# State products of a bidirectional S5 layer: factors as weights and chunk inputs moving, in place of chunk inputs as weights

## The chip, the cores and the metric

The kernel runs on one core of a Trainium2 chip. The metric is the device time of one execution in microseconds. Three runs of the kernel before took 1600.52, 1600.65 and 1602.56 us (median 1600.65).

## The reference

Two layers of a backbone over 256 latent tokens and 256 context tokens with 1024 channels, all fp32. Layer 0 mixes tokens with a bidirectional diagonal state space (S5), 64 groups of 16 channels with 64 complex states each, and then runs a dense SwiGLU; layer 1 is attention and a top-2-of-8 expert SwiGLU. The change lies in the S5 mixer of layer 0:

```
def _s5_scan(u, a_re, a_im, log_dt, b_re, b_im, s0, reverse):
    lam_re, lam_im, bbar_re, bbar_im = _zoh(a_re, a_im, log_dt, b_re, b_im)
    bu_re = jnp.einsum('bngi,gpi->bngp', u, bbar_re)
    bu_im = jnp.einsum('bngi,gpi->bngp', u, bbar_im)
    ...
    _, _, s_re, s_im = lax.associative_scan(
        _ssm_combine, (a_seq_re, a_seq_im, bu_re, bu_im), reverse=reverse, axis=1)
```

The scan runs over time in both directions (r = 0 forward, r = 1 reverse), context first, then latent tokens. The readout multiplies the states with C, adds a skip term, and a GLU follows.

## The kernel before, in words

Time is cut into 64 chunks of 8 steps. For every chunk and group the kernel computes what the 8 inputs of the chunk add to the state at the end of the chunk (VS), then runs a scan over the 64 chunks on DVE (`scan_range`, L846 to L857), and then computes the outputs from chunk states (`states`, `outer`) and from inputs inside the chunk (`taps`, `windows`, `inner`).

**The inputs.** U (L637 to L642) holds the inputs transposed: 128 partitions (8 steps x 16 channels), 32 slots of 128 columns, 64 columns (chunks) per group.

**The sets.** The 64 groups are worked off in 16 sets of four (`iters`, L570). `z_mul(i)` (L573) forms on DVE three products of lambda powers with B factors, 128 x 512 each (L581). They are the three factors of a complex product with three multiplications; in the sets listed in ZSUM (11 of 16 before) it also adds the first product to the other two (L586). `z_tr(i)` (L589) turns the products with four transposes per factor (L595) and evicts each with ACT into zz (L596): two factors in a ZSUM set, three otherwise. `v_stage(i)` (L652) multiplies: weights are 64 chunk columns of U, and 256 columns of zz move (L662; in a set without sums also the first factor, L661). ACT evicts into vc (L663). `t_stage(i)` (L666) turns vc with four transposes (L674), and ACT evicts the result into VS, the forward half with L677 and the reverse half with two L680.

**What runs beside it.** `w_gen(blk)` (L684) is a generator of 22 DVE pieces, two of 128 x 512 (L687, L689) and twenty of 128 x 1024 (L701 to L709), which form the readout weights W of one half of the groups, in two tensors (wr by L703 and L707, wi by L705 and L709). The list WN says how many pieces are taken in each iteration. FILL lists the eight iterations in which one slice of the modulation matrix is multiplied (`ada_go`: L264 on PE, evicted into R by L270). In the next iteration `ada_done` turns R with four transposes (L284, tile cp), ACT gathers it into part (L285), and after the last of the eight slices DVE reduces part into cols (L290, L292).

**The order.** The loop of L714 issues in iteration i: z_mul(i) and z_tr(i) for i from 2 to 15, ada_done, v_stage(i - 1), t_stage(i - 2), WN[i] pieces of W, ada_go. After it `pin` (L93) fixes the order of the instructions on DVE, ACT and PE as they were issued. Sets 0 and 1 are multiplied and turned before the loop. zq and zz have two buffers each, PSUM eight tiles of 128 x 512.

**Behind the loop.** The pools z (zq, zz, vc) and f are closed, and W1, the readout weights of the second half, is opened at the other end of the same memory. POOL loads dm (L744) into the place of pool f, DVE multiplies it (L746) and runs w_gen(1), and then `scan_range` starts (L888): per chunk L852, L855 and L857, each on the result of the one before. Taps on PE (L779, L784) run beside that.

Of the kernel before, what the change touches and what calls it, by code (L numbers as in the profile page):

```python
# [10 lines left out]
F32 = mybir.dt.float32  # L11
# [3 lines left out]
AF = mybir.ActivationFunctionType  # L15
# [30 lines left out]
WOP = ((13, 13, 17, 17, 18, 19, 20, 20, 21, 21, 22, 22, 24, 24, 24, 24), (29, 29, 30, 30, 31, 32, 33, 34, 35, 35, 36, 36))  # L46
FILL = (3, 5, 6, 7, 9, 10, 11, 13)
LATE = 8
ZSUM = (4, 5, 6, 8, 9, 10, 11, 12, 13, 14, 15)
WN = (0, 6, 1, 2, 1, 1, 2, 2, 2, 2, 1, 4, 2, 1)  # L50


def host_consts():
# [26 lines left out]
def backbone_kernel(ctx: ExitStack, tc: tile.TileContext, x, c, cx, c_ctx, ada_w, ada_b, norm_mix_g, norm_ffn_g,  # L80
# [4 lines left out]
    V, S, T, GP, SY = nc.vector, nc.scalar, nc.tensor, nc.gpsimd, nc.sync  # L85
# [42 lines left out]
    def popen(name, bufs, side):  # L128
        cm = tc.tile_pool(name=name, bufs=bufs, side=side, reuse_waits="tile")
        opened.append(cm)  # L130
        return cm.__enter__(), cm
# [11 lines left out]
    def ps(name="ps"):  # L143
        return ps_pool.tile([128, 512], F32, tag="ps", name=name)
# [45 lines left out]
    z, z_cm = popen("z", 2, "left")  # L190
# [24 lines left out]
    ident = kc[:, 0:128]  # L215
# [89 lines left out]
    def ada_go(ld_=None):  # L305

        if ld_ is None:
            ld_, = ada_next(1)
        ada_open.append((ld_, ada_ev(ada_mm(ld_))))

    def ada_done(late=None):
        while ada_open:
            ada_turn(*ada_open.pop(0), late)
# [17 lines left out]
    for r in range(2):  # L331
        src = bn[:, r].rearrange("g r (p i) -> g (r p) i", i=I)
        for q in range(2):
            t = ps()
# [235 lines left out]
    iters = [(blk, gp) for blk in range(2) for gp in range(8)]  # L570
    zst = {}

    def z_mul(i):  # L573

        blk, gp = iters[i]
        g0 = 32 * blk + 4 * gp
        gs = slice(g0, g0 + 4)
        qs_ = []
        for k, (a, b) in enumerate(((PS_, BB[0]), (PZ[1], tb[1]), (PZ[0], tb[0]))):
            q = z.tile([128, 4, 8, I], F32, name=f"zq{k}", tag=f"zq{k}")  # L580
            V.tensor_tensor(q, a.rearrange("p s g -> p g s")[:, gs, :, None].to_broadcast([128, 4, 8, I]),  # L581
                            b[:, gs, None, :].to_broadcast([128, 4, 8, I]), op=OP.mult)
            qs_.append(q)
        if i in ZSUM:
            for k in (1, 2):
                V.tensor_tensor(qs_[k], qs_[k], qs_[0], op=OP.add)  # L586
        zst[i] = qs_

    def z_tr(i):  # L589
        qs_ = zst[i]  # L590
        zz = z.tile([128, 3, 4, 128], F32, name="zz")
        for k in range(1 if i in ZSUM else 0, 3):
            t = ps()
            for g in range(4):
                T.transpose(t[:, 128 * g:128 * g + 128], qs_[k][:, g].rearrange("p s i -> p (s i)"), ident)  # L595
            S.activation(zz[:, k].rearrange("p g q -> p (g q)"), t, AF.Copy)  # L596
        zst[i] = zz
# [6 lines left out]
    t = ps()  # L604
    T.transpose(t[:, :128], pr, ident)
    S.activation(pcol, t[:, :128], AF.Copy)
    t = ps()
# [22 lines left out]
    for r in range(2):  # L630
        for q in range(2):
            t = ps()
# [5 lines left out]
    for q in range(8):  # L638
        t = ps()
# [9 lines left out]
    VS = s_pool.tile([128, 64, 2, G], F32, name="VS", tag="big")  # L649
    w0, w0_cm = popen("w0", 1, "right")  # L650
    W = [[w0.tile([128, 32, 9, I], F32, name=f"W0{r}") for r in range(2)], None]
    def v_stage(i):  # L652
        blk, gp = iters[i]
        zz = zst[i]
        vc = z.tile([128, 2, 2, 128], F32, name="vc")
        t = ps()
        for g in range(4):
            o = t[64 * (g % 2):64 * (g % 2) + 64, 256 * (g // 2):256 * (g // 2) + 256]
            u = U[:, 8 * g + gp, 64 * blk:64 * blk + 64]
            if i not in ZSUM:  # L660
                T.matmul(o, lhsT=u, rhs=zz[:, 0:1, g, :].to_broadcast([128, 2, 128]), start=True, stop=False)  # L661
            T.matmul(o, lhsT=u, rhs=zz[:, 1:3, g, :], start=(i in ZSUM), stop=True)  # L662
        S.activation(vc.rearrange("p g r q -> p (g r q)"), t, AF.Copy)  # L663
        zst[i] = vc

    def t_stage(i):  # L666
        blk, gp = iters[i]
        g0 = 32 * blk + 4 * gp
        vc = zst.pop(i)
        t = ps()  # L670
        for r in range(2):
            for g in range(2):
                o = 256 * r + 128 * g
                T.transpose(t[:, o:o + 128], vc[:, g, r], ident)  # L674
        tv = t.rearrange("p (r g c) -> p r g c", r=2, g=4)
        vs = VS[:, :, :, g0:g0 + 4].rearrange("p c r g -> p r g c")
        S.activation(vs[0:64], tv[0:64], AF.Copy)  # L677
        for h in range(2):
            a = tv[64:128, :, :, 32 * h + 31:32 * h + 32]
            S.activation(vs[64:128, :, :, 32 * h:32 * h + 32],  # L680
                         bass.AP(tensor=a.tensor, offset=a.offset, ap=[a.ap[0], a.ap[1], a.ap[2], [-1, 32]]), AF.Copy)
# [29 lines left out]

    wgen = w_gen(0)
    n = len(iters)
    for i in range(n + 2):  # L714
        if 2 <= i < n:
            z_mul(i)
            z_tr(i)
        ada_done()
        if 0 <= i - 1 < n:
            v_stage(i - 1)  # L720
        if 0 <= i - 2 < n:
            t_stage(i - 2)
        for _ in range(WN[min(i, len(WN) - 1)]):
            next(wgen, None)
        if i in FILL:
            ada_go()
# [12 lines left out]
    for zz in range(2):  # L739
        rs = slice(64 * zz + 32, 64 * zz + 48)  # L740
        for blk in range(2):
            for gh in range(2):
                o = 512 * blk + 256 * gh + 128 * zz
# [512 lines left out]
    for j in range(2):  # L1256
        for lt in range(2):
# [3 lines left out]
            tv = tab[:, j, lt].rearrange("p o (a j d) -> p o j a d", a=2, j=2)  # L1261
# [33 lines left out]
    for kt in range(KT):  # L1295
        if kt == 2:
            later()
        for j, w in enumerate(w0):
            for tt in range(4):
                o = pts[tt][:, 256 * j:256 * j + 256]  # L1300
                T.matmul(o, lhsT=h[0][:, kt, 128 * tt:128 * tt + 128], rhs=w[0][:, kt, :], start=(kt == 0 and j == 0),
                         stop=False)
                T.matmul(o, lhsT=h[0][:, kt, 128 * tt:128 * tt + 128], rhs=w[1][:, kt, :], start=False, stop=False)
                T.matmul(o, lhsT=h[1][:, kt, 128 * tt:128 * tt + 128], rhs=w[0][:, kt, :], start=False,
                         stop=(kt == KT - 1 and j == 1))
# [377 lines left out]
    n = len(items)  # L1683
# [393 lines left out]
    n = len(chunks)  # L2077
# [49 lines left out]
    with tc.If(nmax > 128):  # L2127
        op_, op_cm = popen("op", 1, "right")
        for e_ in range(NE):
# [8 lines left out]
            for q in range(2):  # L2138
                t = ps()
                for j in range(4):  # L2140
                    for lt in range(2):
                        T.matmul(t[:, 128 * j:128 * j + 128],
                                 lhsT=hf[:, lt, 512 * q + 128 * j:512 * q + 128 * j + 128], rhs=se[:, lt, :],
                                 start=(lt == 0), stop=(lt == 1))
                S.activation(xg[:, 4 * q:4 * q + 4, :].rearrange("p a b -> p (a b)"), t, AF.Copy)
            yp = [ps("py") for _ in range(2)]
            for f in range(DFF // 256):
                t = ps()
                for half in range(2):
                    w = load(moe_gu[0, e_].rearrange("(k p) n -> p k n", p=128)[:, :, DFF * half + 256 * f:  # L2150
                                                                                  DFF * half + 256 * f + 256], [KT, 256])
                    for kt in range(KT):
                        T.matmul(t[:, 256 * half:256 * half + 256], lhsT=xg[:, kt, :], rhs=w[:, kt, :],
                                 start=(kt == 0), stop=(kt == KT - 1))
# [3 lines left out]
                t = ps()  # L2158
# [5 lines left out]
                for j in range(2):  # L2164
                    for n in range(2):
                        T.matmul(yp[n], lhsT=aT[:, 128 * j:128 * j + 128], rhs=w[:, j, 512 * n:512 * n + 512],
                                 start=(f == 0 and j == 0), stop=(f == DFF // 256 - 1 and j == 1))
            so = op_.tile([128, 256], F32, name="so")
            t = ps()
# [3 lines left out]
            for n in range(2):  # L2173
                y, u = [op_.tile([128, 512], F32, name=t_) for t_ in ("y", "u")]
                S.activation(y, yp[n], AF.Copy)
                for lt in range(2):
                    t = ps()
# [37 lines left out]
```

## Time and profile before

| what | value |
|---|---|
| median of three runs | 1600.65 us |
| the profiled execution | 1599.54 us, its span 1597.8 us |
| PE busy | 1482.7 us (93%) |
| DVE busy | 894.0 us (56%) |
| ACT busy | 708.4 us (44%) |
| the loop over sets | about 61 to 136 us |
| the scan over chunks | about 159 to 234 us |

The span is the time from the first to the last instruction; the execution's own time is 1.74 us longer. PE's busy time counts matmuls, whose ends are modelled: consecutive matmuls overlap in it, so the cost of one in a stream is read from starts, not from durations. PEld are the weight loads.

### The profile page before, as it was taken

How to read it: one execution, taken by the hardware profiler on the slowest of the kernel's cores; microseconds unless marked ns; L12 is line 12 of the kernel's file. 1: busy time of each engine (PE TensorE's matmuls, PEld its weight loads, DVE VectorE, ACT ScalarE, POOL GpSimd, SP SyncE). 2: the span in 40 equal slices, each digit the busy share in tenths (PEclk: the TensorE clock that was granted, in tenths of full speed). 3: DMA queues.
4: the chain of work that ended last, by engine and by line, in shares of the span. 5: the costliest groups of instructions: out<-in, count | busy, mean ns of one | idle time of the engine just before them, and what ended most of it. 6: DMA issues, size and time to landing. Idle time of an engine off the chain costs nothing.

```text
span 1597.8 us, 24082 instructions
## 1 busy us (share of the span) xinstructions
PE 1482.7 (93%) x9742; PEld 1046.3 (65%) x9742; DVE 894.0 (56%) x1391; ACT 708.4 (44%) x928; POOL 38.6 (2%) x69
## 2 busy tenths in 40 slices
PE   4897859999999999999899899989998999989995
PEld 3454648768888888878767687447843786357641
DVE  6997994354232333246877876337831785168621
ACT  4687674243212222235575665136621573056500
POOL 1001000000000000001001000000000000000020
PEclk9997889999999999999999899999999999999999
DMA  9682567263232321234442779999999999999996
GB/s 263 228 307 88 157 181 237 79 211 109 95 113 79 106 97 61 87 127 151 168 172 99 245 225 378 405 407 408 406 406 404 409 405 393 403 409 404 402 405 246
DMA packets 167192, 398.49 MB, mean 249 GB/s; under 512 B 12108, under 2 KB 66576, under 8 KB 166944
## 3 DMA queue, kind: packets, MB, share of 16 engines
q1 hardware_dynamic: 164688, 391.61, 66.5%
q0 software_dynamic: 1184, 3.18, 0.8%
q10 hardware_dynamic: 1200, 2.07, 0.6%
q8 instruction: 79, 1.29, 0.3%
q14 instruction: 41, 0.34, 0.1%
HBM read 394.78 MB, written 2.05 MB: 248 GB/s over the span
## 4 chain that ended last, share of the span: by engine, by line
PE 77%; DVE 10%; DMA 5%; ACT 4%; issue 1%; SPq 0%; DVEq 0%; ACTq 0%
PE pgu L982 10%; PE pgu L981 10%; PE pgu L983 10%; PE pgu L1932 8%; DMA raw<-in_moe_w_gate_up_dram 3%; PE pd L981 3%; PE pd L983 3%; PE pd L982 3%; PE py L981 3%; PE py L982 3%; PE py L1995 3%; PE py L983 3%; DVE sq L852 2%; DVE VS L857 1%; DVE sq L855 1%
## 5 line engine op out<-in xcount | busy, mean ns | idle before, releaser
L962 DVE TENSOR_TENSOR lo<-raw,hi 128x2048 fp32r<-128x2048 f32 (+1 forms) x184 | 401.0, 2186 | 209.1 <-ACT hi L962 206.9
L962 ACT ACTIVATE hi<-raw 128x2048 fp32r<-128x2048 f32 (+1 forms) x184 | 337.4, 1834 | 314.0 <-PE pd L982 81.1
L1932 PE MATMUL pgu<-raw,xb 128*32 128x512 f32 (+1 forms) x1536 | 157.0, 558 | 2.1 <-DMA raw<-in_moe_w_gate_up_dram 2.1
L981 PE MATMUL pgu<-hi,xa 128*128 128x512 f32 (+1 forms) x384 | 148.2, 386 | 5.3 <-ACT hi L962 5.3
L982 PE MATMUL pgu<-lo,xa 128*128 128x512 f32 (+1 forms) x384 | 147.2, 383 | 5.5 <-DVE lo L962 5.5
L983 PE MATMUL pgu<-hi,xa 128*128 128x512 f32 (+1 forms) x384 | 146.1, 381 | 0.0
L981 PE MATMUL pgu<-hhi,hi 128*128 128x512 f32 x352 | 137.0, 390 | 0.5 <-ACT hhi L1113 0.5
L982 PE MATMUL pgu<-hlo,hi 128*128 128x512 f32 x352 | 137.1, 389 | 0.0
L983 PE MATMUL pgu<-hhi,lo 128*128 128x512 f32 x352 | 137.0, 389 | 0.0
L1932 PEld LDWEIGHTS pgu<-raw,xb 128*32 128x32 f32 x1536 | 48.4, 110 | 98.7 <-issue 86.6
L981 PEld LDWEIGHTS pgu<-hi,xa 128*128 128x128 f32 x384 | 74.6, 194 | 23.7 <-ACT hi L962 6.0
L982 PEld LDWEIGHTS pgu<-lo,xa 128*128 128x128 f32 x384 | 74.5, 194 | 19.2 <-DVE lo L962 6.4
L1995 PE MATMUL py<-raw,aT 128*32 128x512 f32 x704 | 80.1, 594 | 5.6 <-DMA raw<-in_moe_w_down_dram 5.5
L983 PEld LDWEIGHTS pgu<-hi,xa 128*128 128x128 f32 x384 | 74.3, 193 | 13.8
L981 PEld LDWEIGHTS pgu<-hhi,hi 128*128 128x128 f32 x352 | 66.0, 188 | 15.0 <-ACT hhi L1113 1.4
L982 PEld LDWEIGHTS pgu<-hlo,hi 128*128 128x128 f32 x352 | 66.1, 188 | 14.5 <-DVE ncq L1110 0.8
L983 PEld LDWEIGHTS pgu<-hhi,lo 128*128 128x128 f32 x352 | 66.1, 188 | 13.7
L981 PE MATMUL pd<-act,hi 128*128 128x512 f32 x176 | 70.0, 399 | 0.0
L983 PE MATMUL pd<-act,lo 128*128 128x512 f32 x176 | 69.5, 395 | 0.0
L982 PE MATMUL pd<-act,hi 128*128 128x512 f32 x176 | 69.5, 395 | 0.0
L981 PE MATMUL py<-hi,aT 128*128 128x512 f32 x176 | 69.2, 393 | 0.0
L982 PE MATMUL py<-lo,aT 128*128 128x512 f32 x176 | 69.0, 392 | 0.0
(444 smaller groups left out, 2346.6 us busy)
## 6 DMA issues: line engine op xcount, KB each, us to landing
raw<-in_moe_w_gate_up_dram SPq DMA_DIRECT2D x128, 1024.0 KB, 11.4
raw<-in_moe_w_down_dram SPq DMA_DIRECT2D x88, 1024.0 KB, 10.5
raw<-in_ada_w_dram SPq DMA_DIRECT2D x48, 1024.0 KB, 7.5
raw<-in_moe_w_gate_up_dram SPq DMA_DIRECT2D x64, 768.0 KB, 9.4
raw<-in_ffn_w_gate_up_dram SPq DMA_DIRECT2D x22, 1024.0 KB, 5.2
raw<-in_ssm_glu_w_dram SPq DMA_DIRECT2D x8, 1024.0 KB, 8.3
raw<-in_ffn_w_down_dram SPq DMA_DIRECT2D x8, 1024.0 KB, 5.1
raw<-in_attn_w_qkv_dram SPq DMA_DIRECT2D x6, 1024.0 KB, 5.1
```

What stands on the lines that cost most here:

```text
L852: V.tensor_tensor(t, VS[:, k - 1, None, :, g].to_broadcast([128, 2, 2, g.stop - g.start]), T8[:, :, :, g], op=OP.mult)
L855: V.tensor_tensor(t[:, :, 0, :], t[:, :, 0, :], t[:, :, 1, :], op=OP.add)
L857: V.tensor_tensor(VS[:, k, :, g], VS[:, k, :, g], t[:, :, 0, :], op=OP.add)
L962: ins = [S.activation(hi, r, AF.Copy), V.tensor_tensor(lo, r, hi.bitcast(F32), op=OP.subtract)]
L981: T.matmul(o, lhsT=a[0], rhs=b[0], start=start, stop=False)
L982: T.matmul(o, lhsT=a[0], rhs=b[1], start=False, stop=False)
L983: T.matmul(o, lhsT=a[1], rhs=b[0], start=False, stop=stop)
L1932: T.matmul(pt[64 * j_ + 32 * q:64 * j_ + 32 * q + 32, 0:bw], lhsT=XB[:, kt, o + 32 * q:o + 32 * q + 32], rhs=wj_[j_][:, kk, b:b + bw], sta ...
L1995: T.matmul(yps[e_][0][64 * n + 32 * q:64 * n + 32 * q + 32, :], lhsT=aT[1][:, m, 32 * q:32 * q + 32], rhs=wt_[0][:, kk, ns], start=first, ...
```

## The change

The state products are formed with the turned factors zz as weights (128 columns) and the 64 chunk columns of U moving, so that the result already has states on partitions. vc, its eviction and t_stage are gone. ACT's first eviction into VS is written in the order chunk, part, group. ZSUM shrinks to four sets. WN is changed so that the pieces of W are taken over all sets. The loop starts at 1 and ends one iteration earlier.

```
-ZSUM = (4, 5, 6, 8, 9, 10, 11, 12, 13, 14, 15)
-WN = (0, 6, 1, 2, 1, 1, 2, 2, 2, 2, 1, 4, 2, 1)
+ZSUM = (9, 11, 13, 15)
+WN = (0, 4, 1, 1, 2, 1, 2, 1, 2, 1, 2, 1, 2, 1)
...
     def v_stage(i):
+
         blk, gp = iters[i]
-        zz = zst[i]
-        vc = z.tile([128, 2, 2, 128], F32, name="vc")
-        t = ps()
+        g0 = 32 * blk + 4 * gp
+        zz = zst.pop(i)
+        tv = ps().rearrange("p (r g c) -> p r g c", r=2, g=4)
         for g in range(4):
-            o = t[64 * (g % 2):64 * (g % 2) + 64, 256 * (g // 2):256 * (g // 2) + 256]
             u = U[:, 8 * g + gp, 64 * blk:64 * blk + 64]
             if i not in ZSUM:
-                T.matmul(o, lhsT=u, rhs=zz[:, 0:1, g, :].to_broadcast([128, 2, 128]), start=True, stop=False)
-            T.matmul(o, lhsT=u, rhs=zz[:, 1:3, g, :], start=(i in ZSUM), stop=True)
-        S.activation(vc.rearrange("p g r q -> p (g r q)"), t, AF.Copy)
-        zst[i] = vc
-
-    def t_stage(i):
-        blk, gp = iters[i]
-        g0 = 32 * blk + 4 * gp
-        vc = zst.pop(i)
-        t = ps()
-        for r in range(2):
-            for g in range(2):
-                o = 256 * r + 128 * g
-                T.transpose(t[:, o:o + 128], vc[:, g, r], ident)
-        tv = t.rearrange("p (r g c) -> p r g c", r=2, g=4)
+                T.matmul(tv[:, :, g, :], lhsT=zz[:, 0, g, :], rhs=u[:, None, :].to_broadcast([128, 2, 64]), start=True,
+                         stop=False)
+            for r in range(2):
+                T.matmul(tv[:, r, g, :], lhsT=zz[:, 1 + r, g, :], rhs=u, start=(i in ZSUM), stop=(i in ZSUM or r == 1))
         vs = VS[:, :, :, g0:g0 + 4].rearrange("p c r g -> p r g c")
-        S.activation(vs[0:64], tv[0:64], AF.Copy)
+        S.activation(VS[0:64, :, :, g0:g0 + 4], tv[0:64].rearrange("p r g c -> p c r g"), AF.Copy)
...
-    for i in range(n + 2):
+    for i in range(1, n + 1):
...
-        if 0 <= i - 1 < n:
-            v_stage(i - 1)
-        if 0 <= i - 2 < n:
-            t_stage(i - 2)
+        v_stage(i - 1)
```

## Rows read from the trace of the kernel before

**Rows 1.** Windows: span and busy us (instructions) of each engine, granted clock, DMA.

```profile
61.00:119.00 58.00, 52.74 (x419) 30.61 (x419) 57.45 (x79) 47.08 (x85) 0.00 (x0) 1.00 0.68 243
...
142.00:159.00 17.00, 16.80 (x132) 11.42 (x132) 16.94 (x17) 10.95 (x33) 0.45 (x4) 0.52 0.10 15
```

**Rows 2.** Chain of waits in order of time: start us, us, engine, tile, line.

```profile
130.16 1.23 PE ps L595 x8
...
157.62 1.14 DVE W L709
...
232.08 0.24 DVE VS L857 x2
```

**Rows 3.** Timeline of DVE and POOL: start us, us, instruction, [idle before and its releaser].

```profile
91.27 1.28 DVE L586 TENSOR_TENSOR zq<-zq,zq 128x512 f32<-128x512 f32 x2
92.47 1.21 DVE L707 TENSOR_TENSOR W<-W,n 128x1024 f32<-128x1024 f32 x1
...
126.93 0.42 DVE L290 TENSOR_REDUCE cols<-part 128x64 f32<-128x256 f32 x1 [5.42 <-ACT part L285]
...
134.11 1.23 DVE L703 TENSOR_TENSOR W<-PQ,CD 128x1024 f32<-128x1024 f32 x1 [3.49 <-PE ps L662]
136.55 1.23 DVE L705 TENSOR_TENSOR W<-PQ,CD 128x1024 f32<-128x1024 f32 x1 [1.22 <-PE ps L674]
...
130.02 4.23 POOL L744 DMA_DIRECT2D dm<-in_ssm_d_dram  x8 [120.06 <-DVE zq L586]
```

**Rows 4.** Timeline of PE, the first product and two stretches of the loop.

```profile
61.02 0.66 PE L661 MATMUL ps<-zz,U 128*64 128x256 f32 x4
...
69.69 1.47 PE L595 MATMUL ps<-kc,zq 128*128 128x128 f32 x12
71.09 0.66 PE L661 MATMUL ps<-zz,U 128*64 128x256 f32 x4
...
79.88 1.04 PE L595 MATMUL ps<-kc,zq 128*128 128x128 f32 x8
80.84 1.08 PE L662 MATMUL ps<-zz,U 128*64 128x256 f32 x8
81.86 0.66 PE L674 MATMUL ps<-kc,vc 128*128 128x128 f32 x4
82.45 1.92 PE L264 MATMUL ada<-raw,sc 128*32 128x512 f32 x16
84.30 1.09 PE L595 MATMUL ps<-kc,zq 128*128 128x128 f32 x8
```

**Rows 5.** Timeline of PE, the end of the loop.

```profile
125.88 0.66 PE L284 MATMUL cp<-kc,R 128*128 128x128 f32 x4 [1.14 <-ACT R L270]
...
131.32 1.08 PE L662 MATMUL ps<-zz,U 128*64 128x256 f32 x8
```

**Rows 6.** Timeline of PE, small streams behind weight loads of 128 and 64 columns.

```profile
171.18 0.71 PE L779 MATMUL ps<-W,bd 128*64 128x144 f32 x8
171.82 0.29 PE L784 MATMUL ps<-dm,kc 16*64 16x16 f32 x4
...
853.71 1.85 PE L1599 MATMUL plt<-rw,xT 128*128 128x8 f32 x16
855.42 0.47 PE L981 MATMUL pw<-hi,oT 128*128 128x512 f32 x1
```

**Rows 7.** Timeline of PE, two gaps and what ran behind the second.

```profile
28.04 3.73 PE L447 MATMUL ps<-ke,L 64*64 64x64 f32 x40 [3.04 <-ACT FT L474]
...
141.90 0.47 PE L779 MATMUL ps<-W,bd 128*64 128x144 f32 x4 [3.59 <-ACT bd L757]
...
153.98 1.11 PE L284 MATMUL cp<-kc,R 128*128 128x128 f32 x4
```

**Rows 8.** Groups by line, shapes kept apart, ACT: busy us, mean ns.

```profile
L677 ACT ACTIVATE VS<-ps 64x512 f32<-64x512 f32 x16 | 17.4, 1089 | 0.0
...
L635 ACT ACTIVATE CT<-ps 128x512 f32<-128x512 f32 x4 | 2.1, 603 | 1.0 <-PE ps L634 1.0
```

## The prediction, blind

> **What bounds the kernel now.** I read the windows first, then the chain of waits, then the timelines of DVE and PE in the stretch that the diff touches. From 61 to 119 us DVE is busy for 57.45 of 58.00 us, PE for 52.74, ACT for 47.08 [rows 1]. That looks like a DVE bound, but the next views say otherwise. The chain runs through the last transposes of set 15 (130.16), then the W products of block 1, which end at 158.76, and then the scan on DVE, one step behind the other to 232.3 us [rows 2]. So what this stage is worth is read at one place: when can the W products of block 1 run through? In DVE's timeline L703 starts at 134.11 after waiting for PE's L662, the state product of set 15, and L705 at 136.55 after waiting for L674, the second turn [rows 3]: the two tensors of W1 lie where the pool z lay. And set 15 itself is late: L290 waits 5.42 us for ACT's part, which waits for PE's cp transposes at 125.88 [rows 3, 5]. DVE had run ahead; PE's order decides the end. Work that leaves DVE is therefore worth nothing unless PE's chain gets shorter as well.
>
> **The change, part by part.** The sum starts at 61.02, PE's first state product [rows 4], and counts PE's instructions in the pinned order.
>
> *Price of a product.* An fp32 product appears as two weight load and matmul pairs. Before, the weights are 64 columns of U and 256 columns move: 8 pairs in 1.02 us (80.84 to 81.86) for a set with sums, and 4 turns in 0.59 (81.86 to 82.45) [rows 4]. After, the weights are 128 columns of zz and 64 (or 128) columns move, so less streams but twice as many columns are loaded. No row has that shape; the nearest is L1599, 128x128 weights with only 8 columns moving: 16 pairs from 853.71 to 855.42, 0.107 us each [rows 6]. From the other side stand the turns, 128 columns loaded and 128 moving: 12 take 1.40, 8 take 0.96, so 0.11 each and 0.08 for the change of shape after them [rows 4]. With 8 or 128 columns moving the pair costs the same; 64 lies between. I take 0.109, ends 0.107 and 0.112. So a set with sums has 4 x 2 products, 16 pairs, 1.74 us, where it had 1.02 + 0.59 = 1.61. A set without has 12 products, 24 pairs, 2.62 us.
>
> [...]
>
> *Sums on DVE.* ZSUM falls from 11 sets to 4. Two additions cost 1.20 us (91.27 to 92.47) [rows 3], so 7 x 1.20 = 8.4 us leave DVE, which was waiting for PE anyway. PE gets 7 x 4 transposes more, 7 x 0.44 = 3.1 us, and the larger product in seven sets, 7 x 8 x 0.109 = 6.1 us. This trade is what makes PE long.
>
> *ACT.* vc's eviction goes (16 times), seven zz evictions come. L677 writes runs of 4 elements instead of single ones: between 0.60 (L635, runs of 16) and the 1.09 it has [rows 8]; I take 1.09. The two L680 move as many elements with the same stride, so about 1.1 again, and R has L635's shape, 0.6: ACT is done with R some 2.8 us after a product, while PE reaches cp after 0.15 + 1.85 (ada, 82.45 to 84.30 [rows 4]) + 1.32 = 3.3 us. So the waits before cp (1.14 us in [rows 5]) vanish. Until 0.4 us more on ACT, nothing of it is on the path. Were the evictions 0.5 us slower after all, some 0.1 x 8 = 0.8 us would come.
>
> *PE up to the last cp.* Products of sets 0 to 12: (11 x 24 + 2 x 16) = 296 pairs x 0.109 = 32.3. Transposes of sets 2 to 14: (10 x 12 + 3 x 8) = 144 x 0.11 = 15.8. Eight ada products at 1.85 + 0.15 for the change of shape ahead (0.59 against 4 x 0.11 [rows 4]) = 16.0. Seven earlier cp of 4 transposes, 0.44 each = 3.1. Together 67.2, so the last cp starts at 61.0 + 67.2 = 128.2, against 125.88. DVE feeds this without a hole: per set it needs three products of the shape of a sum, 1.8 us, and one or two W pieces of 1.14, PE 3.9 or more.
>
> *The end of the loop.* Before, set 15's transposes started 130.16 - 125.88 = 4.28 us after cp [rows 2, 5]. Now one piece of W stands between: the old WN had run all 22 pieces by iteration 11, the new one runs the 22nd in iteration 14, behind L290 and ahead of z_mul(15). It costs 1.14 us [rows 2]. So z_tr(15) starts at 128.2 + 4.28 + 1.14 = 133.6 and takes 1.16 as now (to 131.32 [rows 5]). Then come set 14 without sums and set 15 with: 40 pairs x 0.109 = 4.4, to 139.2. Before, 2.79 us lay between 131.32 and L703, of them 1.02 + 0.59 + 1.02 on PE, so 0.16 is left for the handover: L703 starts at 139.35. With no vc there is no second wait, so L705 follows at 140.5 instead of 136.55. Everything behind is back to back on DVE: **+4.0 us**. I take it that both W1 tensors wait for the last read of zz; if only the first does, L705 runs ahead and 1.14 is saved.
>
> *What follows along.* The dm loads on POOL start after z_mul(15), 130.02 now [rows 3], about 134.4 then; with 4.23 us of issue they are there before L746, which stands four W pieces behind 139.35. No transfer changes its place in a queue. Taps and windows have their own slack behind the scan.
>
> **The sum.** The profiled execution took 1599.54 us, so 1603.5; the median of the three runs shown is 1.1 higher, which would give 1604.6. I say **1604**. The bounds of the terms: 336 pairs at 0.107 to 0.112, -0.7 to +1.0; 0.08 for a change of shape after 14 sets of transposes, 0 to +1.1, ada's 0.15 not needed, -1.2; R's waits, up to +0.8; L705 ahead, -1.1. The likely case spans +1.5 to +6.5 us, 1601 to 1606.5. Anything within 0.2% (3.2 us) cannot be told from no change here.
>
> **Rivals.**
> 1. *Faster.* A pair of 128 loaded and 64 moving columns runs at about 0.08 us, like L779 (64 loaded, 144 moving, 8 pairs from 171.18 to 171.82 [rows 6]). Then 336 x 0.029 = 9.7 us leave PE, L705 starts 5.7 us earlier than now: 1594. It decides below 0.109 - 4.0/336 = 0.097 us a pair. For it: the streams are short. Against: L1599 with 8 columns moving. [...] The turns here cost 110 ns. 13%.
> 2. *The clock.* PE now waits from the end of set 13 (128.2 + 0.44 + 1.74 = 130.4) to 133.6, 3.2 us. A gap of 3.59 before 141.90 was followed by the lower clock (mean 0.52 from 142 to 159), one of 3.04 before 28.04 was not [rows 1, 7]. [...] 9%.
> [...]
> 4. *It does not reach the end*: PE's sum is 2 to 6 us too long, because before it also lost time between instructions that I count in my prices, and the removed second turn pays for the rest: 1598 to 1601. 15%.
>
> **How the numbers follow.** The likely case has 58%; some 70% of it lie above 3.2 us. Slower: 0.41 + 0.09 + 0.05 = 0.55; faster: rival 1 and a little of 4, 0.14; the rest, 0.31, is no change that can be told. The range leaves out rivals 1 and 3: 1598 to 1609.5.
>
> **What would show it.** Right: PE nearly without holes from 61 to 130 us, products L661 to L663 of the new kernel at 0.107 to 0.112 us a pair, DVE with holes in every set, cp of the last ada at about 128, a hole on PE of about 3 us ahead of z_tr(15), L703 waiting for a state product until about 139, the scan starting at about 162.8 instead of 158.76. Wrong: pairs under 0.097 us, or a last cp before 125.9, or W products of block 1 that start while zz is still read.

## The result, and the profile after

The changed kernel took 1609.41 us (median of 20 runs, beside 1600.78 us for the kernel before): 1.0055 times the time before, with an interval of 1.0046 to 1.0064, so 7.4 to 10.2 us slower. The forecast was 1604. Its direction was right and the range just holds the median, but the step forecast was +4.0 us and about twice that came. Its profiled execution took 1610.12 us, 10.6 more than that of before: the first state product starts 0.76 us later, 8.75 us are lost between it and the scan, and the last 1.1 us lie behind the scan's start. So most of it was lost in the stage that the prediction was about, and the whole analysis goes from PE's first state product to DVE's first instruction of the scan: 97.65 us before (61.02 to 158.67), 106.40 after.

PE's timeline of the changed kernel (start us, us, engine, line, tiles, count, and in brackets the idle time before with its releaser):

```profile
61.78 0.39 PE L661 MATMUL ps<-U,zz 128*128 128x128 f32 x2
...
64.41 1.51 PE L595 MATMUL ps<-kc,zq 128*128 128x128 f32 x12
...
129.01 0.60 PE L284 MATMUL cp<-kc,R 128*128 128x128 f32 x4
129.45 1.90 PE L664 MATMUL ps<-U,zz 128*128 128x64 f32 x16
134.47 1.94 PE L595 MATMUL ps<-kc,zq 128*128 128x128 f32 x8 [3.12 <-DVE zq L586]
136.20 0.64 PE L661 MATMUL ps<-U,zz 128*128 128x128 f32 x2
...
140.47 4.37 PE L664 MATMUL ps<-U,zz 128*128 128x64 f32 x20
144.76 1.94 PE L264 MATMUL ada<-raw,sc 128*32 128x512 f32 x8
```

Four readings. The 24 pairs of a set without sums take from 61.78 to 64.41, 0.110 us each. The last cp starts at 129.01, 67.23 us behind the first product. Then comes the hole, 3.12 us, ahead of set 15's transposes. Behind it PE needs 8.56 us (136.20 to 144.76) for 40 pairs, 0.214 each: twice the price of the same pairs at 61.78. (L264 at 144.76 follows the last state product and marks its end.) The windows say why; columns are the stretch, busy us and instructions of PE, weight loads, DVE, ACT, POOL, then the granted clock, the DMA share and GB/s:

```profile
61.00:119.00 58.00, 58.00 (x516) 47.43 (x515) 49.26 (x65) 39.98 (x80) 0.00 (x0) 1.00 0.65 229
132.00:133.00 1.00, 0.00 (x0) 0.00 (x0) 1.00 (x2) 1.00 (x2) 0.00 (x0) 1.00 1.01 377
...
134.00:135.00 1.00, 0.54 (x3) 0.57 (x4) 1.00 (x3) 0.00 (x0) 0.68 (x2) 0.50 0.05 18
142.00:144.00 2.00, 2.00 (x12) 2.00 (x11) 0.00 (x0) 1.07 (x3) 0.00 (x0) 0.50 0.00 0
```

From 61 to 119 us the roles of [rows 1] are exchanged: PE is busy all the time, DVE for 49.26 of 58 us where it was busy for 57.45. Inside the hole the granted clock falls from 1.00 to 0.50, and it is still there at 144. DVE's side of the same stretch, where [rows 3] had L290, L703 and L705:

```profile
130.10 0.42 DVE L290 TENSOR_REDUCE cols<-part 128x64 f32<-128x256 f32 x1 [9.01 <-ACT part L285]
130.55 0.23 DVE L292 TENSOR_TENSOR cols<-cols,pcol 128x64 f32<-128x64 f32 x1
130.69 1.22 DVE L698 TENSOR_TENSOR W<-n,W 128x1024 f32<-128x1024 f32 x1
131.83 0.68 DVE L581 TENSOR_TENSOR zq<-PS,BB 128x512 f32<-128x512 f32 x1
...
144.93 1.23 DVE L692 TENSOR_TENSOR W<-PQ,CD 128x1024 f32<-128x1024 f32 x1 [8.87 <-PE ps L664]
146.07 1.22 DVE L694 TENSOR_TENSOR W<-PQ,CD 128x1024 f32<-128x1024 f32 x1
...
168.18 0.42 DVE L838 TENSOR_TENSOR sq<-VS,T 128x256 f32<-128x256 f32 x1
```

L692 and L694 are the old L703 and L705, and L838 is the first instruction of the scan. DVE waits 9.01 us for the last modulation slice, then runs the moved piece of W (L698, between L292 and the factors of set 15), and then waits 8.87 us for the last state product. The list of waits (engine, tile, line, releaser, us in total, times, longest) shows where the 8.4 us of additions that left DVE went. The row of L581, the factors of the sets, before and after:

```profile
DVE zq L581 <- PE ps L595: 0.5, 1, 0.5
DVE zq L581 <- PE ps L595: 9.5, 6, 2.2
```

They became waits of DVE for PE's transposes: 9.0 us more in this row.

### The profile page after: what moved, and what is told of

Read it like the earlier page. It is cut to its first block, busy times and chain, and to the rows that moved or that the text cites. A ratio compares the mean times of both kernels' runs of the same rounds, so it can differ in the third digit from the quotient of the medians.

```text
span 1608.3 us, 24356 instructions
## 1 busy us (share of the span) xinstructions
PE 1501.9 (93%) x9890; PEld 1077.9 (67%) x9890; DVE 885.3 (55%) x1377; ACT 696.2 (43%) x919; POOL 38.2 (2%) x69
## 4 chain that ended last, share of the span: by engine, by line
PE 79%; DVE 9%; DMA 5%; ACT 2%; issue 1%; SPq 0%; DVEq 0%; ACTq 0%
PE pgu L968 10%; PE pgu L967 10%; PE pgu L969 10%; PE pgu L1918 8%; DMA raw<-in_moe_w_gate_up_dram 3%; PE pd L967 3%; PE pd L969 3%; PE pd L968 3%; PE py L967 3%; PE py L968 3%; PE py L1981 2%; PE py L969 2%; DVE sq L838 2%; PE ps L664 2%; PE ada L264 1%; DVE VS L843 1%
```

## The experiments

All times from the first state product to the scan, each from its own profile, with the ratio of the run times to the kernel before:

| kernel | us to the scan | ratio | interval |
|---|---|---|---|
| before | 97.65 | 1 | |
| changed | 106.40 | 1.0055 | 1.0046 to 1.0064 |
| e1, piece of W earlier | 104.23 | 1.0039 | 1.0027 to 1.0052 |
| e2, cols behind the loop | 98.22 | 1.0017 | 1.0000 to 1.0035 |
| e3, new product alone | 98.68 | 1.0012 | 1.0002 to 1.0022 |
| e4, hole filled | 101.68 | 1.0031 | 1.0018 to 1.0044 |
| e5, before, cols behind the loop | 96.50 | 0.9997 | 0.9985 to 1.0010 |
| e6, new product alone, cols behind | 92.73 | 0.9980 | 0.9971 to 0.9990 |
| e7, new sets and WN alone | 103.21 | 1.0042 | 1.0022 to 1.0063 |
| e8, as e6 with W spread | 90.29 | 0.9972 | 0.9961 to 0.9982 |
| e9, before, one piece of W late | 100.01 | 1.0053 | 1.0034 to 1.0072 |
| e10, as e8 with nine sets | 91.94 | 0.9983 | 0.9962 to 1.0005 |
| e11, e8 again | 90.31 | 0.9968 | 0.9957 to 0.9979 |
| e12, as e7, piece earlier | 100.49 | 1.0036 | 1.0016 to 1.0057 |

The theory after the result: the hole ahead of set 15's transposes halves the clock, and that is the difference between forecast and measurement. The first rival to it: the new products are slow at the loop's end for another reason.

### e4: the hole filled

```
+        if i == n - 2:
+            idle = ps()
+            for j in range(28):
+                T.transpose(idle[:, 128 * (j % 4):128 * (j % 4) + 128], ident, ident)
```

The lines stand behind `v_stage(i - 1)` in the loop of the changed kernel, so the 28 turns follow the products of set 13, where the hole was; they go into a tile that nobody reads.

> 28 turns of the identity into an unread PSUM tile are put behind the products of set 13, 3.1 us of PE work in the place of the hole; nothing waits for less. Theory (the clock falls because PE stands idle in the hole): set 15's transposes start as late as in the changed kernel, but the 48 pairs after them run at 0.11 us instead of 0.2: 4.8 us earlier, about 1604.6. Rival (the clock is lost whatever fills the hole): no change, 1609.

PE's timeline and the window of this kernel:

```profile
131.53 3.23 PE L712 MATMUL ps<-kc 128*128 128x128 f32 x28
134.82 1.23 PE L595 MATMUL ps<-kc,zq 128*128 128x128 f32 x8
...
140.39 1.92 PE L264 MATMUL ada<-raw,sc 128*32 128x512 f32 x16
```

```profile
130.00:141.00 11.00, 10.94 (x100) 10.16 (x102) 6.37 (x10) 5.37 (x11) 4.22 (x8) 1.00 0.46 162
```

The transposes of set 15 start no earlier than without the filler (72.69 us behind the first product in both), and nothing else is changed, but the clock stays at 1.00 and the 40 pairs take 4.51 us instead of 8.56. The scan starts 4.72 us earlier (106.40 to 101.68); in the run times the ratio falls from 1.0055 to 1.0031, 3.8 us. So the lower clock cost about 4.7 us, and without it the stage takes 4.03 us more than before: the +4.0 of the forecast.

### e1 and e2: a smaller hole, and none

e1 takes the 22nd piece of W one iteration earlier, ahead of L290; e2 takes L290 and L292 out of the loop and puts them behind it, so that set 15's factors don't stand behind DVE's wait for the last modulation slice.

```
e1
-WN = (0, 4, 1, 1, 2, 1, 2, 1, 2, 1, 2, 1, 2, 1)
+WN = (0, 4, 1, 1, 2, 1, 2, 1, 2, 1, 2, 1, 2, 2)
e2
+    shut = []
...
-        ada_done()
+        ada_done(shut)
...
+    for f in shut:
+        f()
```

> The 22nd W piece is taken in iteration 13, so it no longer stands between L292 and z_mul(15). Theory (the chain cp, part, cols, z_mul(15) makes a hole on PE, and the lower clock comes out of that hole): set 15's transposes start 4.3 us after cp instead of 5.46, the hole shrinks from 3.1 to 2.0 us, as long as the one of the kernel before, the clock stays at its upper level, and the scan starts 1.2 + 4.8 = 6 us earlier than in the changed kernel: about 1603.5. Rival (short streams behind full weight loads lose the clock whatever the hole is): only 1.2 us earlier, products of sets 14 and 15 still at 0.2 us a pair: about 1608.

> The two DVE instructions that wait for ACT's part (L290, L292) are issued behind the loop, so z_mul(15) no longer waits for cp. Theory: no hole at all on PE, set 15's transposes follow the products of set 13 at once, clock at its upper level to the end of the loop, last product ends near 136.5 instead of 144.8, scan 8.3 us earlier: about 1601, the kernel before within 0.1%. Rival (clock lost by the short streams themselves): the hole goes, -3.1, but the last products still run at half rate: about 1606.

e1, PE's timeline and the window behind the hole:

```profile
133.45 1.23 PE L595 MATMUL ps<-kc,zq 128*128 128x128 f32 x8 [1.98 <-DVE zq L586]
```

```profile
134.00:136.00 2.00, 2.00 (x15) 1.98 (x14) 0.00 (x0) 1.14 (x2) 2.00 (x5) 0.73 0.21 46
```

The hole shrank as meant, to 1.98 us, but the clock fell all the same, some 1.5 us into the transposes and products behind it (a mean of 0.73 from 134 to 136, 0.50 from 136 to 144). Only 2.17 us of about 6 came back: a miss of my expectation, which had put the limit by the holes of the kernel before alone. Its time, 1608.06 us, is the one that the expectation gave to the rival, short streams that lose the clock whatever the hole is; it takes e2 to decide between the two. e2, PE's and DVE's timelines:

```profile
131.54 1.05 PE L595 MATMUL ps<-kc,zq 128*128 128x128 f32 x8
...
134.66 2.34 PE L664 MATMUL ps<-U,zz 128*128 128x64 f32 x20
```

```profile
137.10 1.23 DVE L692 TENSOR_TENSOR W<-PQ,CD 128x1024 f32<-128x1024 f32 x1 [5.97 <-PE ps L664]
```

No hole, the granted clock is 1.00 from 119 to 140 us, and the products keep their price to the end (20 pairs in the row at 134.66 take 2.34 us, in the changed kernel 4.37): 8.18 us come back. With the new products and no hole the clock stayed up, so both rivals (slow for another reason, and the short streams) are out.

### e3: the new product alone

The changed kernel with the old lists:

```
+ZSUM = (4, 5, 6, 8, 9, 10, 11, 12, 13, 14, 15)
+WN = (0, 6, 1, 2, 1, 1, 2, 2, 2, 2, 1, 4, 2, 1)
```

> The new state product alone, with the 11 sum sets and the piece list of the kernel before. Theory (the exchange of 7 sum sets for transposes and third products is what made PE long; the product itself costs 1.74 instead of 1.61 us in a sum set): PE gets 7 x (0.44 + 0.87) = 9.2 us less than the changed kernel, DVE runs without holes to about 118, the last product ends near 130, the scan starts near 153 instead of 158.8: about 1595, faster than both. Rival (the new product is the cost, the sets do not matter): near the changed kernel, 1607 to 1609.

PE's timeline and the window at the loop's end:

```profile
66.79 2.74 PE L595 MATMUL ps<-kc,zq 128*128 128x128 f32 x12 [1.78 <-DVE zq L581]
...
128.89 1.94 PE L595 MATMUL ps<-kc,zq 128*128 128x128 f32 x8 [1.93 <-DVE zq L586]
130.62 6.93 PE L664 MATMUL ps<-U,zz 128*128 128x64 f32 x32
```

```profile
128.00:130.00 2.00, 1.11 (x6) 1.14 (x7) 1.34 (x3) 0.66 (x2) 1.26 (x3) 0.58 0.99 369
```

Another miss: forecast as faster than before, it came out at 1.0012. It has two holes of under 2 us, ahead of set 2 and ahead of set 15, and the clock falls at both (0.50 from 68 to 70 and from 130 to 138): the 12 transposes at 66.79 take 2.74 us (the 12 at 64.41 in the changed kernel 1.51), the 32 pairs 6.93. The shorter chain of the new product was spent on that.

### e5 and e6: L290 behind the loop, with either product

Both have e2's edit; e5 in the kernel before, e6 in e3 (new product, old ZSUM and WN).

> The kernel before, with L290 and L292 issued behind the loop and nothing else. Theory (cols stands between cp and z_mul(15) in both kernels): its hole of 2.0 us ahead of set 15's transposes goes, the scan starts 2 us earlier than before, about 1599. Rival (the hole only covers a wait for something else, as ACT): no change, 1601.

> The new product with the 11 sum sets and the piece list of before, and L290 and L292 behind the loop. Theory (without a hole at the end the clock stays up, and in a sum set the product is worth its turn): the 40 pairs behind set 13 take 4.5 us instead of 8.6 and start 2 us earlier than in the run with the old sets alone: last product near 131.3, scan near 154.7, about 1597, faster than the kernel before by 0.2 to 0.3%. Rival (the clock falls even so, since the stream is short everywhere): near 1601 to 1603.

e5, DVE's timeline:

```profile
133.30 1.23 DVE L703 TENSOR_TENSOR W<-PQ,CD 128x1024 f32<-128x1024 f32 x1 [2.86 <-PE ps L662]
135.97 1.23 DVE L705 TENSOR_TENSOR W<-PQ,CD 128x1024 f32<-128x1024 f32 x1 [1.45 <-PE ps L674]
```

e6, PE's and DVE's:

```profile
127.69 3.93 PE L664 MATMUL ps<-U,zz 128*128 128x64 f32 x32
131.55 1.92 PE L264 MATMUL ada<-raw,sc 128*32 128x512 f32 x16
```

```profile
131.71 1.23 DVE L692 TENSOR_TENSOR W<-PQ,CD 128x1024 f32<-128x1024 f32 x1 [3.15 <-PE ps L664]
132.85 1.22 DVE L694 TENSOR_TENSOR W<-PQ,CD 128x1024 f32<-128x1024 f32 x1
```

With the old product the edit gives 1.15 us in the stage and nothing that can be told in the time: the wait for the second turn (L674) still stands between the two W1 tensors. With the new product it gives 5.95 us against e3, and the kernel is faster than before (0.9980): 32 pairs take 3.86 us, L694 follows L692 at once.

### e7, e9 and e12: which hole loses the clock

e7 is the kernel before with the new ZSUM and WN; e12 is e7 with the last number of WN raised to 2, as in e1; e9 is the kernel before with its last piece of W moved into iteration 14.

```
e7
+ZSUM = (9, 11, 13, 15)
+WN = (0, 4, 1, 1, 2, 1, 2, 1, 2, 1, 2, 1, 2, 1)
e9
+WN = (0, 6, 1, 2, 1, 1, 2, 2, 2, 2, 1, 1, 0, 0, 1)
e12
+WN = (0, 4, 1, 1, 2, 1, 2, 1, 2, 1, 2, 1, 2, 2)
```

> The old product with its second turn, with the 4 sum sets and the piece list of the changed kernel. Theory (the exchange of sum sets is what makes PE long): PE gets 7 x (0.44 + 0.91) = 9.5 us more than before and loses some 4 to 5 us of waits, the piece ahead of z_mul(15) costs 1.1 more: scan 5 to 7 us later than before, 1606 to 1608, as slow as the changed kernel without its loss of clock. Rival (the new product is the cost): within 2 us of the kernel before.

> The kernel before with its last W piece but nothing else moved to iteration 14, between L292 and z_mul(15), where the changed kernel has it. Theory (the piece lies on the chain that ends the loop): set 15's transposes start 5.4 instead of 4.3 us after cp, the hole on PE grows from 2.0 to 3.1 us, the scan starts 1.1 us later: 1602.5 if the clock stays up. If the hole alone, with streams of 256 columns around it, is enough to lower the clock, the 24 pairs behind it cost another 1.5 to 3 us: 1604 to 1605. Rival (the piece is hidden): 1601.

> The exchange of sets with the old product (e7), and the 22nd piece of W taken in iteration 13 as in e1: the hole ahead of the transposes of set 15 shrinks from 3.64 us by one piece (1.14) to about 2.5. It tells apart why a hole of 1.98 in e1 was followed by the lower clock and one of 2.02 in the kernel before was not. Theory A, what PE does around the hole counts (the new products): with the old products the clock stays at 1.00 from 130 to 138, set 15's transposes take 1.23 as one group, L703 starts about 75.9 us after the first product (78.6 in e7: 1.14 for the piece and some 1.6 for the clock less), and first product to scan takes about 100.5 (103.2 in e7), some 1605. Theory B, the hole alone counts, and one of about 2 us falls on either side: with 2.5 the clock falls to 0.50 within two us of the transposes' start, L703 starts about 77.5 after the first product, and first product to scan takes about 102.1, some 1607.

e7, PE's timeline and a window:

```profile
133.78 1.46 PE L595 MATMUL ps<-kc,zq 128*128 128x128 f32 x8 [3.64 <-DVE zq L586]
```

```profile
134.00:138.00 4.00, 4.00 (x22) 2.46 (x22) 1.37 (x2) 1.19 (x2) 3.86 (x8) 0.58 0.10 16
```

e9, PE's timeline and windows:

```profile
131.50 1.23 PE L595 MATMUL ps<-kc,zq 128*128 128x128 f32 x8 [3.16 <-DVE zq L586]
```

```profile
134.00:136.00 2.00, 2.00 (x10) 1.01 (x8) 0.00 (x0) 0.95 (x2) 1.59 (x4) 0.50 0.16 16
136.00:138.00 2.00, 1.50 (x12) 0.78 (x8) 0.97 (x1) 1.96 (x4) 0.00 (x0) 0.96 0.04 6
```

e12, PE's timeline and the window:

```profile
132.52 1.23 PE L595 MATMUL ps<-kc,zq 128*128 128x128 f32 x8 [2.50 <-DVE zq L586]
```

```profile
134.00:136.00 2.00, 2.00 (x20) 1.36 (x16) 0.00 (x0) 0.61 (x2) 2.00 (x5) 1.00 0.16 24
```

With the old product, the clock falls to 0.50 behind holes of 3.64 and 3.16 us and is 1.00 from 130 to 140 around one of 2.50; with the new one, it falls to 0.50 behind 1.98 (e1). So the length of the hole alone doesn't tell. e12 was to tell whether what PE runs around it does, and its stage came out at the 100.5 us that this theory gave, against 102.1 for the rival. One trace of each kernel does not settle that: in the last section, one kernel, traced twice, loses the clock behind a hole once and keeps it once, with the length and the instructions the same. That the new product makes the clock easier to lose is therefore not shown, and e12's agreement can be luck. e9 shows that one piece of W in the wrong place costs the kernel before 2.36 us in the stage, 1.14 for the piece and, by subtraction, some 1.2 for the clock. Its four runs scatter from 1600.3 (the profiled one) to 1613.5, so the stage is read from it and not the ratio. And e7 shows that the new sets and the new WN cost about as much without the new product as with it: 1.0042 against 1.0055, with intervals that overlap.

### e8, e10 and e11: a version that beats both

e8 is e6 with W's pieces spread away from iteration 1; e10 has nine sets with sums in it; e11 is e8 once more.

```
e8
+ZSUM = (4, 5, 6, 8, 9, 10, 11, 12, 13, 14, 15)
+WN = (0, 4, 2, 2, 1, 1, 2, 2, 2, 2, 1, 2, 1, 1)
e10
+ZSUM = (5, 8, 9, 10, 11, 12, 13, 14, 15)
```

> As the run with the new product, the old sum sets and L290, L292 behind the loop, but four W pieces instead of six ahead of set 2, so that set 2's transposes do not wait for DVE. Theory (the hole of 1.8 us ahead of set 2 starts the lower clock at 67 us there): no hole and no lower clock at 67, but DVE is the one that is full in the middle, so the end moves by 0 to 2 us: 1595 to 1597. Rival (PE is what is full): 4 us earlier, 1593.

> As the run with the old sum sets, late L290 and L292 and four first pieces, but sets 4 and 6 without sums: 2 x 1.2 us less on DVE, 2 x (0.44 + 0.87) us more on PE. Theory (PE's order decides the end): 2.6 us later than with eleven sets, about 1599. Rival (DVE, full from 61 to 122 us, decides): up to 2.4 us earlier, 1594.

> The run with the old sum sets, late L290 and L292 and four first pieces once more, in five rounds, for its size: 0.997 of the kernel before, 4 to 5 us faster.

e8, the window, and DVE's timeline at the loop's end:

```profile
61.00:119.00 58.00, 57.63 (x505) 45.92 (x507) 57.93 (x79) 41.75 (x83) 0.00 (x0) 1.00 0.72 257
```

```profile
128.41 1.23 DVE L692 TENSOR_TENSOR W<-PQ,CD 128x1024 f32<-128x1024 f32 x1 [3.14 <-PE ps L664]
```

From 61 to 119 us PE and DVE are both busy nearly all the time, no hole is left ahead of set 2, and the scan starts 7.4 us sooner than before, counted from the first product. Twice measured: 0.9972 and 0.9968, 4.5 to 5.1 us. Not all of the 7.4 us reaches the end: in the two profiled executions (1599.54 and 1595.35) 0.4 us are lost ahead of the first product and 2.8 behind the scan's start; this was not followed up. e10, the window:

```profile
61.00:119.00 58.00, 58.00 (x516) 47.27 (x515) 57.16 (x78) 40.83 (x81) 0.00 (x0) 1.00 0.67 236
```

Two sets less with sums make PE's stage 1.65 us longer, in the direction that PE's price of a set gives and less than expected; its run times scatter from 1593.6 to 1609.7, so its ratio does not settle which is better. In its profiled execution, which took 1609.73, the granted clock is 0.50 all the way from 784 to 812 us, where e8 has 0.89 and e11 1.00: that lies in layer 1, far behind the edited stage.

## Why the prediction was right and wrong

Its sum can be read against the trace in four marks, each in us from the first state product:

| mark | before | forecast | after |
|---|---|---|---|
| last cp (L284) | 64.86 | 67.2 | 67.23 |
| transposes of set 15 | 69.14 | 72.6 | 72.69 |
| second tensor of W1 (old L705, new L694) | 75.53 | 79.5 | 84.29 |
| scan | 97.65 | 101.65 | 106.40 |

The prediction's 162.8 for the scan adds its 4.0 us to 158.76, the end of the last W product. The scan's first instruction starts at 158.67, so on this mark the forecast is 101.65.

*Price of a product: right.* 24 pairs take 2.63 us (61.78 to 64.41), 0.110 each, forecast 0.109. Rival 1 (under 0.097) is out. No run shows the longer pair that rival 3 counted on, with 0.05 in the sum of the chances; what they show in its place is 0.110 for the new product and 0.11 for the turns, with 128 columns loaded and 128 moved [rows 4].

*PE up to the last cp: right.* 67.23 against 67.2. DVE's 8.4 us were worth nothing, as the prediction said: they came back as waits for PE. e7 shows it without the new product.

*The waits before cp: right.* No L284 row at the loop's end carries a bracket any more, where [rows 5] had 1.14 us behind R. The eviction that I took at 1.09 us was off the path, but it takes 0.59, my lower bound:

```profile
64.61 0.59 ACT L666 ACTIVATE VS<-ps 64x512 f32<-64x512 f32 x1 [1.87 <-PE ps L664]
```

*The end of the loop: right up to the transposes of set 15.* The piece of W stands where it was forecast (130.69, between L292 and L581), from cp to the transposes it takes 5.46 us, forecast 5.42, and the hole is 3.12 us, forecast 3.2. L692 waits for the last product and L694 follows at once, with no second wait.

*The step that failed: rival 2, the clock, put at 9% and set beside the likely case instead of on top of it.* The forecast for the stretch behind the hole was 6.85 us (1.16 for the transposes, 4.4 for 40 pairs, 0.15 of handover, 1.14 for L692); it took 11.60 (134.47 to 146.07), because the transposes took 1.73 and the pairs 8.56. That is 4.75 us more, and e4, which takes the lower clock away and nothing else, gives back 4.72. The rival had the place and the hole right, and the price too: I put it at some 5 us for the 48 pairs left, so 1609, an estimate from four transposes that take 0.66 us at a granted clock of 1.00 and 1.11 at 0.50 [rows 5, 7]. Only its chance was wrong. I had weighed a hole of 3.2 against two others, 3.59 with and 3.04 without a fall [rows 1, 7], and gone by the nearer one. That one was misread. The clock column shows 1.00 behind it, but 16 pairs of L264 that follow take 3.64 us there, and the next 16 take 1.92; PE's timeline of the kernel before, with a later hole:

```profile
32.62 3.64 PE L264 MATMUL ada<-raw,sc 128*32 128x512 f32 x16
...
37.98 1.92 PE L264 MATMUL ada<-raw,sc 128*32 128x512 f32 x16
...
918.01 1.97 PE L1965 MATMUL pat<-kc,a 128*128 128x128 f32 x8 [3.15 <-DVE a L1944]
```

By its prices PE ran at half rate at 33 us, whatever the column shows, so the hole of 3.04 is no evidence for a clock that stays up. The one of 3.15 ahead of 918.01 is nearer to 3.2 and was not weighed: from 918 to 920 us the granted clock is 0.50. In that trace, from 60 us on, every hole on PE of 2.80 us or more began at 1.00 and was followed by 0.50: 2.80 ahead of 885.29, 3.15, 3.59 ahead of 141.90, 5.44 ahead of 194.07 and 11.29 ahead of 228.32. Shorter ones go either way: with the new product the clock fell to 0.50 behind 1.98 us (e1), with the old one it stayed at 1.00 behind 2.50 (e12). And the hole itself was a certain part of my own sum. So a fall deserved much more than an even chance, and with its price of 5 us added to the sum the forecast would have been 1609.

*Rival 4* (a sum for PE that is 2 to 6 us too long) is out by the first mark. Behind L694 nothing was given back either: it takes 22.11 us to the scan, as the 22.12 from L705 before.

By parts, in the stage: the longer chain on PE up to the last cp costs 2.37 us, cp to the transposes of set 15 1.18 more (the piece of W), the rest up to the second tensor of W1 would be 6.85 instead of 6.39, 0.46 more, and the clock adds 4.75; 8.76 together.

## What to carry to other kernels

Work taken from an engine that runs ahead is worth nothing while the engine that it then waits for gets longer; ask of each instruction moved which wait it now stands behind, and who is waiting for what stands behind it. When a sum leaves a hole on PE (here 3.12 us, behind which the clock cost 4.7), price what follows at the lower clock as an addition to the sum, not as another story; hold a clock that a view shows against the price of instructions that are found again elsewhere; and look first for an edit that takes the hole away: L290 and L292 moved behind the loop were worth 8.2 us here, and together with the new product, the old sets and W spread it made the stage 7.4 us shorter than before.

## What the runs showed of the hardware that was not expected

*Holes of one length can go either way.* The kernel before has one of 2.48 us ahead of set 2 and one of 2.02 ahead of set 15; PE's timeline:

```profile
65.50 1.83 PE L595 MATMUL ps<-kc,zq 128*128 128x128 f32 x12 [2.48 <-DVE zq L581]
...
130.16 1.23 PE L595 MATMUL ps<-kc,zq 128*128 128x128 f32 x8 [2.02 <-DVE zq L586]
```

The granted clock stays at 1.00 there (62 to 68 and 128 to 136 us), as behind the 2.50 us of e12, all three among old products. Behind 1.78 and 1.93 (e3) and 1.98 us (e1), among new ones, it fell to 0.50. It is tempting to put this down to the products. But e8 and e11, one kernel traced twice, have the same hole of 1.68 us in layer 1, between the same instructions; PE's timeline and a window, first of e8, then of e11:

```profile
780.82 0.63 PE L1420 MATMUL pt<-kc,pr 128*128 128x128 f32 x4 [1.68 <-DVE pr L1414]
784.00:786.00 2.00, 1.36 (x5) 0.71 (x4) 2.00 (x8) 2.00 (x6) 0.00 (x0) 0.50 0.00 0
```

```profile
781.37 0.63 PE L1420 MATMUL pt<-kc,pr 128*128 128x128 f32 x4 [1.68 <-DVE pr L1414]
784.00:786.00 2.00, 1.00 (x6) 0.42 (x4) 2.00 (x9) 1.69 (x4) 0.00 (x0) 1.00 0.00 0
```

The clock falls to 0.50 in e8 and stays at 1.00 in e11. Ahead of 56 us, in code that no edit touches, it differs as well: the mean of the granted clock from 0 to 56 is 1.00 in the kernel before, which has a hole of 2.31 us at 42, and in e4, and 0.97 in e1, e2 and e3. So the same hole between the same instructions goes either way from one execution to the next, and what decides was not found.

*An eviction into runs of four elements* (L666, 64x512) takes 0.59 us, as long as one into runs of 16 (L635, 0.60), where single elements take 1.09 [rows 8].
